# A hybrid diffusion backbone on one core: TensorE's list scheduler separates transposes, and the first stage's code is reordered

## The chip, the cores and the metric

The kernel runs on 1 core of a Trainium2 chip. Its time is the device time of one execution in microseconds; lower is better. The profile is one execution taken by the hardware profiler on that core.

## The reference, cut to what matters

Two layers, each an adaLN-modulated RMS norm, a wide input projection, three token mixers (RG-LRU, chunkwise retention, latent attention) and a gated merge. 256 latent tokens and 256 context tokens go through the same weights; D_MODEL is 1024. What the change touches is how the first lines are scheduled, and every transpose of the program.

```python
def _layer(x, xc, c, c_ctx, lp, rope_ret, rope_mla, with_ctx):
    mod = jax.nn.silu(c) @ lp['w_mod'] + lp['b_mod']
    mod_c = jax.nn.silu(c_ctx) @ lp['w_mod'] + lp['b_mod']
    shift, scale, gate = jnp.split(mod, 3, axis=-1)
    shift_c, scale_c, gate_c = jnp.split(mod_c, 3, axis=-1)
    h = _rms(x, lp['norm_gain']) * (1.0 + scale[:, None]) + shift[:, None]
    hc = _rms(xc, lp['norm_gain']) * (1.0 + scale_c) + shift_c
    (xa, ga, qb, kb, vb, gb, qd, kvd, kr, gc, gm) = _split_cols(h @ lp['w_in'])
    ...
    x = x + (gate[:, None] * _merge(lp, ya, yb, yc, ga, gb, gc, gm)).astype(x.dtype)
```

## The kernel before, in words

**Arithmetic.** Every f32 matrix is split into a rounded high part and a remainder, `hi` and `lo` (an ACT copy and a DVE subtraction), and each product is three matmuls (hi·hi, hi·lo, lo·hi, `mm3`). A matmul has a 128x128 stationary operand and 128 to 512 moving columns. A transpose is a TensorE instruction too: the data is the stationary operand, the identity (`ident`) moves, 128 columns. In the trace a transpose reads `mm<-ident,sm` or `mm<-ident,t`.

**Order.** Nothing is issued as it is written. All operations are recorded (`Recorder.add`), and `Recorder.schedule` then runs a list schedule over the five engines: each engine, when its modelled busy time is over, takes the ready operation that was recorded first (its `prio`), if the buffers that it writes are free within the windows of `WINDOW`, `FIRST` and `RESERVE`. The model's prices are in `_cost`; a transpose counts 107 ns there, a 512-column matmul 216 ns. The result is a fixed order per engine, which `emit` writes out at line 369; so nearly all instructions carry that one line. On the chip each engine works through its own order, and waits where an operand is not there.

**First stage.** Four blocks c = 0 to 3. `mod_pe` multiplies four weight tiles of `wmod` with the conditioning vector (`mm<-t,cz`, 16 instructions a block), ACT copies the bank, four small matmuls with `sel` bring the columns back (`mm<-sel,sm`), and DVE makes `sh` and `gt` from them (`put_columns`). `norm_begin` makes the normalized rows, each of four token tiles once; `norm_channels` transposes two channel tiles of a block (`mm<-ident,t`), scales them with `gt` and `sh` into `sm` and splits them into `hx`. `kv_project` of the block then multiplies `hx` with that block's split `wkv` tile (24 matmuls of 320 columns, `mm<-whi,hx` and `mm<-wlo,hx`). `rope_tables` loads two small tables (`mrope`, `grope`) and multiplies them into four tables `rt`; it stands behind the four blocks. All loads go out on SP's queue in the scheduled order. `t` in the trace is a buffer of the pool `t2` (21 buffers of 128x1024), used for the rows, the `wmod` tiles and most intermediates.

**Later.** Latent attention of layer 0 (about 40 to 200 us), LRU, retention and merge (to 870 us), latent attention of layer 1 (870 to 1000 us), then the rest. Transposes stand in both attentions (keys, queries, probabilities), in the retention heads, at the modulation of layer 1, at the norm between the layers and in the last merge.

Of the kernel before, what the change touches and what calls it, by code (L numbers as in the profile page):

```python
# [22 lines left out]
NTT = TOK // 128  # L23
# [128 lines left out]
class Recorder:  # L152
# [72 lines left out]
    def schedule(self):  # L225
# [28 lines left out]
        def switch(op):  # L254
            return op.table is not None and op.table != table[0]

        t = 0.0
        evn = 0
        left = len(ops)
        while left:  # L260
            progressed = True
            while progressed:
                progressed = False
                for e in engines:
                    if busy[e] > t:
                        continue
                    w = wait[e]
                    while w and w[0][0] <= t:
                        _, pr, k, op = heapq.heappop(w)
                        heapq.heappush(avail[e], (pr, k, op))  # L270
                    a = avail[e]
                    hold = []
                    pick = None
                    while a:
                        item = heapq.heappop(a)
                        op = item[2]
                        ok = True
                        need = {}
                        for b in op.allocs:
                            if b.live:  # L280
                                continue
                            need[b.tag] = need.get(b.tag, 0) + 1
                            spare = (FIRST if b.tag == "mm" and b.seq < 24 else RESERVE).get(b.tag, 0) if b.seq > nxt[b.tag] + need[b.tag] - 1 else 0
                            if free[b.tag] < need[b.tag] + spare or b.seq > nxt[b.tag] + WINDOW.get(b.tag, 0):
                                ok = False
                        if ok and pick is not None:
                            if not switch(op):
                                hold.append((pick.prio, id(pick), pick))
                                pick = op
                                break  # L290
                            ok = False
                        elif ok:
                            pick = op
                            if not switch(op):
                                break
                            limit = op.prio + SWITCH
                            continue
                        hold.append(item)
                        if pick is not None and item[0] > limit:
                            break  # L300
                    for item in hold:
                        heapq.heappush(a, item)
                    if pick is None:
                        continue
                    op = pick
                    for b in op.allocs:
                        if not b.live:
                            b.live = True
                            free[b.tag] -= 1
                            q = self.tags[b.tag]["queue"]  # L310
                            while nxt[b.tag] < len(q) and q[nxt[b.tag]].live:
                                nxt[b.tag] += 1
                    cost = op.cost
                    if switch(op):
                        cost += 1283.0
                        table[0] = op.table
                    op.start = t
                    busy[e] = t + cost
                    op.end = t + cost + op.lag
                    order.append(op)  # L320
                    left -= 1
                    evn += 1
                    heapq.heappush(events, (busy[e], evn, None))
                    evn += 1
                    heapq.heappush(events, (op.end, evn, op))
                    for s in op.succs:
                        if s.engine == e and e != "SP":
                            s.ready = max(s.ready, busy[e] + SELF[e])
                        else:
                            s.ready = max(s.ready, op.end + _latency(e, s.engine))  # L330
                        s.npred -= 1
                        if s.npred == 0:
                            heapq.heappush(wait[s.engine], (s.ready, s.prio, id(s), s))
                            evn += 1
                            heapq.heappush(events, (s.ready, evn, None))
                    progressed = True
            if not left:
                break
            if not events:
                self.stuck(nxt, free, wait, avail)  # L340
            t2, _, op = heapq.heappop(events)
            t = max(t, t2)
            batch = [op]
            while events and events[0][0] <= t:
                batch.append(heapq.heappop(events)[2])
            for op in batch:
                if op is not None:
                    for b in op.bufs:
                        b.users -= 1
                        if b.users == 0:  # L350
                            free[b.tag] += 1
# [97 lines left out]
def tile_hybrid(ctx, tc, ins, out):  # L449
# [265 lines left out]
        V.scalar_tensor_tensor(t, t, 1.0, ps, op0=ALU.add, op1=ALU.mult)  # L715
        return t

    def rope_tables(l):
        tabs = []
        mrope = small()[:, 0:384]  # L720
        S.dma_start(mrope, ins["mrope"])
        mrope = mrope.rearrange("p (a s d) -> p a s d", a=2, s=3)
        grope = small()[:, 0:128]
        S.dma_start(grope, ins["grope"][l])
        grope = grope.rearrange("p (a d) -> p a d", a=2)
        for i in range(2):
            for j in range(2):
                t = rec.tile(f"rt{i}{j}", [128, 3, 64], F32)
                V.tensor_tensor(t, mrope[:, j], grope[:, i:i + 1, :].to_broadcast([128, 3, 64]), op=ALU.mult)
                tabs.append(t)  # L730
        return tabs
# [459 lines left out]
    xn = {}  # L1191

    lat = Latents(0, None)
    xs = []
    for tt in range(NTT):
        xs.append(big(F32))
        S.dma_start(xs[tt], ins["xin"][tt])
    wm = {}
    for c in range(4):
        wm[c] = [big(F32) for _ in range(4)]  # L1200
        for kp in range(4):
            S.dma_start(wm[c][kp], ins["wmod"][0, 4 * c + kp])
        wkv = load_raw(ins["wkv"][0, c], 640)
        if c == 0:
            for tt in range(NTT):
                xn[tt] = norm_begin(xs[tt])
        mod_pe(0, c, wm, gt, sh)
        for kt in (2 * c, 2 * c + 1):
            norm_channels(xn, kt, gt, sh, hh, hl)
        lat.kv_project((c,), {c: wkv})  # L1210
    lat.tabs = rope_tables(0)
    sp = cload("sp", [128, DEPTH, 24])
    rrope = cload("rrope", [128, 2, 256])
    toep = cload("toep", [128, 384])
# [40 lines left out]
    for l in range(DEPTH):  # L1255
# [8 lines left out]
        hold = {}  # L1264
# [189 lines left out]
```

## Time and profile before

| | |
|---|---|
| median of 3 runs | 1396.25 us (1396.11 to 1398.47) |
| the profiled execution | 1396.45 us, of it the span 1394.1 us |
| TensorE (PE) | busy 1375.3 us, 99% of the span, 6926 matmuls |
| VectorE (DVE) | busy 1026.6 us, 74% |
| ScalarE (ACT) | busy 801.3 us, 57% |
| granted TensorE clock | 0.999 of full speed |
| HBM read | 167.86 MB, 121 GB/s over the span |

Matmuls are pipelined: the start of one and the modelled end of the one before overlap. So a duration of a matmul in the trace (some 390 ns for 512 columns) is not what it costs. The cost is read from the distance of starts, over a few instructions that are known by name.

### The profile page before, as it was taken

The numbers are of one execution on the slowest core, as the hardware profiler recorded it, in microseconds if no ns is written. First come the engines' busy times: TensorE is split into PE (matmuls) and PEld (weight loads), VectorE is DVE, ScalarE is ACT, GpSimd is POOL, SyncE is SP. The second block draws the span as 40 slices with busy tenths as digits, with TensorE's granted clock in tenths as the row PEclk, the third lists the DMA queues.
The fourth block names the chain that finished last, engine by engine and source line by source line (L and its number), as shares of the span: only waits on it lengthen the run. The fifth ranks groups of instructions, "written<-read, shape, count | busy, mean of one in ns | idle before, by whom it ended". The sixth has DMA issues, their size and how long they took to land.

```text
span 1394.1 us, 19215 instructions
## 1 busy us (share of the span) xinstructions
PE 1375.3 (99%) x6926; PEld 1162.4 (83%) x6926; DVE 1026.6 (74%) x2067; ACT 801.3 (57%) x1597; POOL 86.5 (6%) x109
## 2 busy tenths in 40 slices
PE   6999999999999999999999999999999999999998
PEld 4888888888888888888888888988888888888887
DVE  3699886676669656574884765899778898978755
ACT  4676665776678332153432226877686887945442
POOL 1131110000000000010000001312000000000000
PEclk9999999999999999999999999999999999999999
DMA  9412112223333433413344452333343444564662
GB/s 363 157 48 74 58 62 66 86 91 114 91 114 121 136 98 106 136 51 111 107 142 143 134 179 69 116 94 102 95 123 119 136 151 141 159 194 131 206 182 77
DMA packets 51070, 170.15 MB, mean 122 GB/s; under 512 B 6048, under 2 KB 7840, under 8 KB 50976
## 3 DMA queue, kind: packets, MB, share of 16 engines
q1 hardware_dynamic: 50976, 168.93, 38.4%
q8 instruction: 54, 0.88, 0.3%
q14 instruction: 40, 0.33, 0.1%
HBM read 167.86 MB, written 1.05 MB: 121 GB/s over the span
## 4 chain that ended last, share of the span: by engine, by line
PE 92%; DVE 3%; DMA 3%; ACT 1%; issue 0%; POOL 0%; SPq 0%; ACTq 0%; DVEq 0%; POOLq 0%
PE mm L369 92%; DMA t<-in_wmod_dram 1%; DVE sm L369 1%; DVE t L369 1%; DVE wlo L369 1%; DMA sm<-in_grope_dram 1%; ACT t L369 1%; DVE st L369 0%; DMA raw<-in_wmod_dram 0%; DMA t<-in_xin_dram 0%; ACT sm L369 0%; POOL st L369 0%; SPq L369 0%; ACT whi L369 0%; ACT hx L369 0%
## 5 line engine op out<-in xcount | busy, mean ns | idle before, releaser
L369 PE MATMUL mm<-hx,whi 128*128 128x512 f32 x1664 | 533.3, 393 | 0.0
L369 ACT CAST whi<-raw 128x1024 fp32r<-128x1024 f32 (+4 forms) x280 | 275.7, 995 | 342.6 <-PE mm L369 295.3
L369 DVE TENSOR_TENSOR wlo<-raw,whi 128x1024 fp32r<-128x1024 f32 (+4 forms) x280 | 318.7, 1143 | 143.9 <-ACT whi L369 141.9
L369 PEld LDWEIGHTS mm<-hx,whi 128*128 128x128 f32 x1664 | 309.5, 188 | 60.1
L369 PE MATMUL mm<-hx,wlo 128*128 128x512 f32 (+1 forms) x960 | 342.7, 362 | 0.0
L369 PE MATMUL mm<-whi,t 128*128 128x512 f32 (+1 forms) x656 | 208.9, 383 | 0.4 <-DVE t L369 0.4
L369 PEld LDWEIGHTS mm<-hx,wlo 128*128 128x128 f32 x960 | 180.2, 188 | 29.0
L369 PE MATMUL mm<-whi,hx 128*128 128x512 f32 (+2 forms) x672 | 198.0, 368 | 2.1 <-ACT hx L369 2.1
L369 POOL TENSOR_TENSOR st<-st,nhalf 128x2 f32<-128x2 f32 (+2 forms) x102 | 85.6, 846 | 1221.5 <-DVE st L369 1215.1
L369 PE MATMUL mm<-t,whi 128*128 128x512 f32 x512 | 160.2, 390 | 0.1
L369 PE MATMUL mm<-t,t 128*128 128x256 f32 (+1 forms) x912 | 156.2, 310 | 0.5 <-ACT t L369 0.5
L369 PEld LDWEIGHTS mm<-t,t 128*128 128x128 f32 x912 | 131.5, 189 | 12.9 <-DVE t L369 1.0
L369 PEld LDWEIGHTS mm<-whi,hx 128*128 128x128 f32 x672 | 122.8, 188 | 21.2 <-ACT hx L369 4.2
L369 PEld LDWEIGHTS mm<-whi,t 128*128 128x128 f32 x656 | 121.7, 188 | 18.8 <-DVE t L369 0.6
L369 PE MATMUL mm<-wlo,t 128*128 128x512 f32 (+1 forms) x328 | 125.4, 382 | 0.0
L369 PE MATMUL mm<-wlo,hx 128*128 128x512 f32 (+2 forms) x336 | 123.1, 368 | 0.0
L369 PEld LDWEIGHTS mm<-t,whi 128*128 128x128 f32 x512 | 95.9, 188 | 20.4 <-DVE t L369 0.5
L369 PE MATMUL mm<-t,wlo 128*128 128x512 f32 x256 | 99.7, 390 | 0.0
L369 ACT CAST t<-sm 128x256 fp32r<-128x256 f32 (+1 forms) x128 | 60.1, 486 | 64.1 <-DVE sm L369 60.8
L369 ACT ACTIVATE sm<-mm 128x128 f32<-128x128 f32 (+4 forms) x242 | 84.0, 364 | 20.8 <-PE mm L369 17.9
L369 ACT CAST t<-mm 128x256 fp32r<-128x256 f32 (+1 forms) x138 | 61.9, 471 | 30.9 <-PE mm L369 30.1
L369 DVE TENSOR_TENSOR t<-mm,t 128x512 fp32r<-128x512 f32 (+2 forms) x138 | 71.3, 530 | 8.2 <-ACT t L369 7.1
(106 smaller groups left out, 1507.9 us busy)
## 6 DMA issues: line engine op xcount, KB each, us to landing
raw<-in_wu_dram SPq DMA_DIRECT2D x224, 512.0 KB, 3.7
raw<-in_wmod_dram SPq DMA_DIRECT2D x32, 512.0 KB, 3.7
t<-in_wmod_dram SPq DMA_DIRECT2D x16, 512.0 KB, 9.6
t<-in_xin_dram SPq DMA_DIRECT2D x8, 512.0 KB, 6.4
raw<-in_wup_dram SPq DMA_DIRECT2D x8, 512.0 KB, 4.0
raw<-in_wlru_dram SPq DMA_DIRECT2D x16, 256.0 KB, 3.1
raw<-in_wqd_dram SPq DMA_DIRECT2D x8, 384.0 KB, 4.0
raw<-in_wup_dram SPq DMA_DIRECT2D x8, 384.0 KB, 3.4
```

Of the source, the lines that this page charges most:

```text
L369: getattr(eng[op.engine], op.method)(*[r(x) for x in op.args], **{k: r(v) for k, v in op.kwargs.items()})
```

## The change

Two parts. In `schedule`, TensorE remembers whether its last instruction was a transpose (`turned`). If it was, the first transpose that comes up is set aside (`stash`) and the search goes on among the ready operations; the transpose is taken if nothing else can go. A transpose that does not follow a transpose is priced at 30 ns in the model in place of 107. In the first stage, the two rope tables' loads (now one buffer, `rope_load`) are recorded ahead of the rows, `norm_begin` behind all `wmod` and `wkv` loads, and the projection of block c behind the modulation and norm of block c + 1.

```diff
+        turned = False
@@
                     pick = None
+                    stash = None
                     while a:
                         item = heapq.heappop(a)
                         op = item[2]
@@
+                        elif ok and e == "PE" and turned and op.method == "transpose":
+                            if stash is None:
+                                stash = item
+                            else:
+                                hold.append(item)
+                            continue
                         elif ok:
                             pick = op
@@
                     for item in hold:
                         heapq.heappush(a, item)
+                    if stash is not None:
+                        if pick is None:
+                            pick = stash[2]
+                        else:
+                            heapq.heappush(a, stash)
@@
                     cost = op.cost
+                    if e == "PE":
+                        if op.method == "transpose" and not turned:
+                            cost = 30.0
+                        turned = op.method == "transpose"
@@
-    def rope_tables(l):
+    def rope_load(l):
+        t = small()
+        S.dma_start(t[:, 0:384], ins["mrope"])
+        S.dma_start(t[:, 384:512], ins["grope"][l])
+        return t
+
+    def rope_tables(l, t=None):
         tabs = []
-        mrope = small()[:, 0:384]
-        S.dma_start(mrope, ins["mrope"])
-        mrope = mrope.rearrange("p (a s d) -> p a s d", a=2, s=3)
-        grope = small()[:, 0:128]
-        S.dma_start(grope, ins["grope"][l])
-        grope = grope.rearrange("p (a d) -> p a d", a=2)
+        t = t or rope_load(l)
+        mrope = t[:, 0:384].rearrange("p (a s d) -> p a s d", a=2, s=3)
+        grope = t[:, 384:512].rearrange("p (a d) -> p a d", a=2)
@@
     lat = Latents(0, None)
+    rload = rope_load(0)
     xs = []
@@
-    wm = {}
+    wm, wkv = {}, {}
     for c in range(4):
         wm[c] = [big(F32) for _ in range(4)]
         for kp in range(4):
             S.dma_start(wm[c][kp], ins["wmod"][0, 4 * c + kp])
-        wkv = load_raw(ins["wkv"][0, c], 640)
-        if c == 0:
-            for tt in range(NTT):
-                xn[tt] = norm_begin(xs[tt])
+        wkv[c] = load_raw(ins["wkv"][0, c], 640)
+    for tt in range(NTT):
+        xn[tt] = norm_begin(xs[tt])
+    for c in range(4):
         mod_pe(0, c, wm, gt, sh)
         for kt in (2 * c, 2 * c + 1):
             norm_channels(xn, kt, gt, sh, hh, hl)
-        lat.kv_project((c,), {c: wkv})
-    lat.tabs = rope_tables(0)
+        if c:
+            lat.kv_project((c - 1,), wkv)
+    lat.kv_project((3,), wkv)
+    lat.tabs = rope_tables(0, rload)
```

What that does to the fixed orders is shown at three places. Counted over the whole of TensorE's order, there are 522 transposes before and after. Before they stand in 169 runs (6 of one transpose, 105 of two, 29 of four, 14 of eight, 15 of other lengths), so that 353 of them follow another transpose. After they stand in 472 runs, 453 of them of one transpose, and 50 follow another. The number of matmuls does not change.

**TensorE, a norm between the layers** (`norm_half`): eight transposes of one row tile, beside matmuls of the next output rows (`hx` is the stationary operand there, `whi` and `wlo` the split weights). Before:

```order
L369 MATMUL mm<-t_6912,whi 128x512 x2
L369 MATMUL mm<-t_6912,wlo 128x512
L369 MATMUL mm<-ident,t_6360 128x128 x8
L369 MATMUL mm<-hx,whi 128x512 x2
L369 MATMUL mm<-hx,wlo 128x512
L369 MATMUL mm<-hx,whi 128x512 x2
```

After, the same eight transposes begin behind the same matmul, with one 512-column matmul between each two:

```order
L386 MATMUL mm<-t_6909,whi 128x512 x2
L386 MATMUL mm<-t_6909,wlo 128x512
L386 MATMUL mm<-ident,t_6359 128x128
L386 MATMUL mm<-hx,whi 128x512
L386 MATMUL mm<-ident,t_6359 128x128
L386 MATMUL mm<-hx,whi 128x512
L386 MATMUL mm<-ident,t_6359 128x128
L386 MATMUL mm<-hx,wlo 128x512
L386 MATMUL mm<-ident,t_6359 128x128
L386 MATMUL mm<-hx,whi 128x512
```

The run of eight became eight runs of one; the matmuls in between are those that stood behind the run.

**VectorE, the first stage**: the four products for `rt` need the rope tables, `st`, `sh` and `gt` are a block's modulation columns, `sm` its scaled channels. Before, in the third block:

```order
L369 TENSOR_TENSOR hx<-sm,hx 128x512 x2
L369 TENSOR_TENSOR rt_384<-sm 128x192
L369 TENSOR_TENSOR st<-mm,cols 128x8
L369 TENSOR_TENSOR wlo<-raw,whi 128x640
L369 COPY sh<-st 128x4
L369 SCALAR_TENSOR_TENSOR gt<-st,cols 128x4
L369 TENSOR_TENSOR rt_404<-sm 128x192
L369 TENSOR_SCALAR sm<-mm,gt,sh 128x256 x2
```

After, the same products stand at the start of the program, ahead of the norm's first operation; the split of the first `wkv` tile (`wlo`) stands ahead of the third row tile's norm (`t_181`):

```order
L386 COPY cz<-cf 128x2x8
L386 TENSOR_TENSOR rt_134<-sm 128x192
L386 TENSOR_TENSOR rt_136<-sm 128x192
L386 TENSOR_TENSOR rt_140<-sm 128x192
L386 TENSOR_TENSOR rt_142<-sm 128x192
L386 TENSOR_SCALAR st<-st 128x1
L386 TENSOR_SCALAR t_156<-t_121,st 128x1024
L386 TENSOR_SCALAR st<-st 128x1
L386 TENSOR_SCALAR t_169<-t_125,st 128x1024
L386 TENSOR_SCALAR st<-st 128x1
L386 TENSOR_TENSOR wlo<-raw,whi 128x640
L386 TENSOR_SCALAR t_181<-t_138,st 128x1024
```

The rope products left the third block, and a wait for a `wkv` tile came into the norm.

**ScalarE, the first stage**: the norms of the four row tiles (`ACTIVATE t,st<-t`), the cast of the first `wkv` tile (`CAST whi<-raw`), and the copy of the first modulation bank (`COPY sm<-mm`). Before:

```order
L369 ACTIVATE t_133,st<-t_117 128x1024
L369 ACTIVATE t_139,st<-t_120 128x1024
L369 ACTIVATE t_146,st<-t_131 128x1024
L369 ACTIVATE t_162,st<-t_136 128x1024
L369 CAST whi<-raw 128x640
L369 COPY sm<-mm 128x512
```

After:

```order
L386 ACTIVATE t_156,st<-t_121 128x1024
L386 ACTIVATE t_169,st<-t_125 128x1024
L386 ACTIVATE t_181,st<-t_138 128x1024
L386 CAST whi<-raw 128x640
L386 ACTIVATE t_195,st<-t_144 128x1024
L386 COPY sm<-mm 128x512
```

The cast moved ahead of the fourth norm. On TensorE the `sel` matmuls of a block's modulation moved from behind the projection of the block before it into that projection (behind its 4th, 11th and 11th matmul for blocks 1, 2 and 3), and the last `cz` matmuls of block 1 moved from behind the projection of block 0 to ahead of it.

## Rows read from the trace of the kernel before

**Rows 1.** The page, part 1: busy time, share, instructions

```profile
PE 1375.3 (99%) x6926; PEld 1162.4 (83%) x6926; DVE 1026.6 (74%) x2067; ACT 801.3 (57%) x1597; POOL 86.5 (6%) x109
```

**Rows 2.** Busy by stretch: length, PE, PEld, DVE, ACT, POOL, clock, DMA share, GB/s

```profile
21.00:38.70 17.70, 14.72 (x107) 10.35 (x105) 8.33 (x21) 7.44 (x14) 0.00 (x0) 1.00 1.04 397
...
85.00:126.40 41.40, 40.39 (x228) 33.69 (x226) 40.09 (x132) 26.33 (x96) 9.47 (x9) 1.00 0.26 79
```

**Rows 3.** Timeline, PE alone, no transposes near: start us, duration us, what

```profile
300.26 0.62 PE L369 MATMUL mm<-hx,whi 128*128 128x512 f32 x2
...
300.94 0.62 PE L369 MATMUL mm<-hx,whi 128*128 128x512 f32 x2
```

**Rows 4.** Timeline, PE alone, around a run of eight transposes

```profile
746.93 0.40 PE L369 MATMUL mm<-t,wlo 128*128 128x512 f32 x1
747.17 1.04 PE L369 MATMUL mm<-ident,t 128*128 128x128 f32 x8
747.96 0.70 PE L369 MATMUL mm<-hx,whi 128*128 128x512 f32 x2
748.50 0.39 PE L369 MATMUL mm<-hx,wlo 128*128 128x512 f32 x1
```

**Rows 5.** Timeline, PE alone, around a run of two

```profile
104.19 0.62 PE L369 MATMUL mm<-hx,whi 128*128 128x512 f32 x2
104.65 0.39 PE L369 MATMUL mm<-hx,wlo 128*128 128x512 f32 x1
104.88 0.38 PE L369 MATMUL mm<-ident,sm 128*128 128x128 f32 x2
105.02 0.71 PE L369 MATMUL mm<-hx,whi 128*128 128x512 f32 x2
105.56 0.40 PE L369 MATMUL mm<-hx,wlo 128*128 128x512 f32 x1
```

**Rows 6.** Timeline, PE and weight loads (PEld), around one transpose between matmuls

```profile
58.31 0.34 PE L369 MATMUL mm<-whi,hx 128*128 128x384 f32 x1
...
58.49 0.27 PE L369 MATMUL mm<-ident,sm 128*128 128x128 f32 x1
58.49 0.19 PEld L369 LDWEIGHTS mm<-whi,hx 128*128 128x128 f32 x1
58.52 0.42 PE L369 MATMUL mm<-whi,hx 128*128 128x384 f32 x1
...
58.77 0.34 PE L369 MATMUL mm<-wlo,hx 128*128 128x384 f32 x1
```

**Rows 7.** The chain that ended last, first 45 us: start us, us, what

```profile
26.93 8.50 DMA sm<-in_grope_dram
...
38.72 6.43 PE mm L369 x45
```

**Rows 8.** Timeline of the first stage, all engines

```profile
9.86 1.06 ACT L369 ACTIVATE t<-t 128x1024 f32<-128x1024 f32 x1
...
15.82 0.72 ACT L369 CAST whi<-raw 128x640 fp32r<-128x640 f32 x1 [4.82 <-DMA raw<-in_wkv_dram]
...
16.64 0.58 ACT L369 COPY sm<-mm 128x512 f32<-128x512 f32 x1
...
21.08 0.39 PE L369 MATMUL mm<-whi,hx 128*128 128x320 f32 x1
...
30.23 0.41 PE L369 MATMUL mm<-whi,hx 128*128 128x320 f32 x1 [0.48 <-ACT hx L369]
...
33.85 0.95 PE L369 MATMUL mm<-sel,sm 128*128 128x2 f32 x8
...
35.22 1.92 PE L369 MATMUL mm<-t,cz 128*32 128x512 f32 x16
```

**Rows 9.** DMA issues, first 45 us: what, count, KB each, median us to landing

```profile
sm<-in_mrope_dram SPq DMA_DIRECT2D x1, 192.0 KB, 9.6
...
sm<-in_grope_dram SPq DMA_DIRECT2D x1, 64.0 KB, 8.5
```

## The prediction

> **What bounds the kernel now.** I read the page first: TensorE is busy 99% of the span and no other engine over 74% [rows 1], at full clock. So time goes where TensorE's order gets longer or shorter, or where TensorE starts later. Then the stretches: before 38.7 us TensorE waits (of 21.0 to 38.7 us it works 14.72 of 17.70), later hardly at all, even between 85 and 126 us, where DVE is busy 40.09 of 41.40 us and TensorE still 40.39 [rows 2]. The chain of waits says the same: ahead of 38.72 us it runs over DMAs, DVE and ACT, at 38.72 us it enters TensorE [rows 7]. So two questions decide: what a transpose costs by itself and in a run, and when TensorE starts its unbroken work.
>
> What an instruction costs is the distance of starts. Three 512-column matmuls take 0.68 us (300.26 to 300.94), 227 ns each [rows 3]. A run of eight: from 746.93 to 748.50 us there are three such matmuls and eight transposes, 1.57 − 0.68 = 0.89 us, **111 ns a transpose** [rows 4]. A run of two: from 104.19 to 105.56 us there are five matmuls and two transposes, 1.37 − 1.135 = 0.235 us, 118 ns each [rows 5].
>
> **Part 1, transposes set apart.** It removes nothing and adds nothing: 522 transposes before and after. It makes 303 runs more (472 less 169). The scheduler's price of 30 ns says that a transpose between matmuls costs 80 ns less. One of the six single transposes before shows what it does cost. From 58.31 to 58.77 us there are two 384-column matmuls and one transpose. The matmul ahead of it takes 0.18 us to the transpose's start (58.49). The next matmul is recorded 0.03 us behind the transpose, which looks like a price of 30 ns; but the one behind that starts only 0.25 us later. Taken over the three, 0.46 − 2×0.175 = **0.11 us** [rows 6]. The same rows show why: the weight load of the matmul behind the transpose starts with the transpose (both 58.49), so what the matmul ahead hid was the transpose's own load, and the load behind is not hidden by a transpose that streams 128 columns only.
>
> So I take no gain from it. What it adds is a border: a run of n costs n×p + f. With p = 109 ns, the eight give f = 0.89 − 0.87 = 0.02 us, the two give 0.235 − 0.218 = 0.017 us, the single one about nothing (0.11 − 0.109). Ends: 0 and 17 ns for each of 303 runs, 0 to 5.2 us. Among the new runs 215 stand behind a 512-column matmul, the rest behind narrower ones like the single one here; and where one matmul alone stands between two transposes (334 places after) two borders share it. I take 5 ns, the side of the row that has the form of the new runs: **+1.5 us**. Below zero, only if a load is hidden that rows 6 show unhidden; that is a rival, below.
>
> The Trainium skill ("TensorE: Matmul & The Clock Gate", section "Part 2: What happens when you issue a matmul") says that weight loads are pulled ahead of matmuls in flight, so that the next tile's weights load while this tile's matmul runs. The trace agrees for the transpose's own load, not for the one behind it (0.11 us for the single transpose [rows 6]). By the page's gap of N/2.4 + 2.5 ns a transpose with both loads hidden would be an estimate of 56 ns, and 303 of them 16 us less.
>
> **Part 2, the first stage.** The rope tables' loads, 192 + 64 KB [rows 9], now stand ahead of the rows and all `wmod` tiles on SP's queue; at 397 GB/s [rows 2] all that follows lands 0.66 us later. In return nothing waits for them at 35.4 us, where they landed (26.93 + 8.50 [rows 7]) and DVE stood ahead of the third block's columns. ACT's order costs more. The cast of the first `wkv` tile waited for its DMA until 15.82 us [rows 8]; now until 16.5, and behind it stand the fourth norm (1.06 us and 0.2 for its sum) and the copy of the first modulation bank, which goes from 16.64 to about 18.8 us. DVE's third and fourth norm wait behind the same tile's split: its cast ends at 17.2, the split and the third norm take 1.6, the fourth norm is ready at some 20.7 us. From there the columns, scaling and cast take 2.8 us, as from the copy's end to the first projection before (17.22 to 21.08, less the `sel`). Projection 0 starts near **23.5** instead of 21.08 us.
>
> Then the moved pieces pay it back. Projection 0 has 24 matmuls, 3.6 us (30.23 to 33.85 [rows 8]), holds block 1's `sel` (0.95 us) and about 0.5 us of wait for the copy: to 28.6. Block 2's `cz` matmuls, 1.92: 30.5. Projection 1 starts there, close to 30.23 before, since its columns came during projection 0. It holds block 2's `sel` and four transposes (3.6 + 0.95 + 0.45): 35.5. Block 3's `cz`, 1.9: 37.4. By then block 2's channels are there (its `sel` ends near 33.1, and columns, scaling and cast take 2.8 to 3 us: 36), and projection 2 starts at **37.4 instead of 38.72 us**. What TensorE has left from there is the same in both (projections 2 and 3, block 3's `sel` and eight transposes, all of the later work). So **−1.3 us**. Ends: −3.0, all that TensorE idles from 21.0 to 38.7 us [rows 2], and +0.7, if the late loads are the last word. The rope products (DVE, 1.3 us) are hidden at the start, where DVE waits for the rows; without that cover they would cost what they cost before.
>
> **The rest of the order** moves with the prices; I find no wait that it adds by name. In the stretch where DVE is full, TensorE loses 1.0 us now [rows 2]; a different interleaving may win that or lose as much again. Middle: 0.
>
> Sum against the profiled execution: 1396.45 − 1.3 + 1.5 = 1396.65 us. Its time lies 0.2 above the median of the three, so in terms of medians **1396.5 us**.
>
> **Rivals.**
> *Hidden transposes.* If a separated transpose costs what its start shows, 30 ns [rows 6], 303 of them save 80 ns each, 24 us: 1396.25 − 24 − 1.3 = 1371 us. For it: the distance between the two starts. Against it: the next distance of the same rows, which gives it all back. This is also the case in which the change does what its price says. The Trainium skill's rule on loads pulled ahead (same page and section as above) stands beside it.
> *A full border.* If each new run costs what the run of two costs between 512-column matmuls, 17 ns [rows 5], that is 5.2 us: 1396.25 − 1.3 + 5.2 = 1400.1 us, slower. It decides from 13 ns a border on (2.8 + 1.3 us over 303). For it: 329 of the 472 runs stand behind 512 columns. Against it: the single transpose with no border to see.
> *The front pays in full.* If projection 2 starts as soon as TensorE's work before it allows, all 3.0 us are won, and with borders at 1 ns it is 1396.25 − 3.0 + 0.3 = 1393.5 us, at the edge of faster. Against it: ACT's late fourth norm.
> *No effect at all*: the front's gain eaten by its later loads, borders free: 1396.9 us, inside the forecast's own range.
>
> **How the numbers follow.** Some 0.2%, 2.8 us, is what a measurement of this kernel can tell from no change. My forecast, between 1393.5 and 1399 us, 0.54; the full border (or a wait that the new order adds in the full stretches) 0.23; the front in full 0.16; hidden transposes 0.07. So faster 0.23, same 0.54, slower 0.23. The range goes from the front in full with the won 1.0 us of the full stretch (1392.5) to the full border with 1.0 lost and the front at nothing (1402.5); hidden transposes lie outside.
>
> **What would show it.** In the changed profile, TensorE's busy share stays 99% and the span within 3 us. Around the norm between the layers, eight transposes and seven matmuls should take 8×0.11 + 7×0.227 = 2.5 us; 1.8 us would say that they are hidden. A matmul's weight load should start with the transpose ahead of it, and not before. The fourth norm on ACT should stand near 17.3 us, projection 0 start near 23.5 and projection 2 near 37.4 us; if projection 0 is as late as that and projection 2 later than 38.7, my paying back is wrong. Wrong altogether would be a span under 1385 us, or new waits on TensorE of over 1 us in the attention stages.

## The result and the profile after

The changed kernel takes **1411.95 us** (median of 4, 1411.88 to 1412.77), the kernel before, run beside it, 1396.58 us (1396.11 to 1398.47). The ratio is **1.0108**, 95% interval 1.0096 to 1.0121: slower by some 15 us, outside the forecast's range. The profiled execution has a span of 1409.8 us against 1394.1, 15.7 us more, at the same clock.

The page, part 1, of the changed kernel, as [rows 1] of before. DVE (1026.6 us before) and ACT (801.3) do the same work; TensorE's share falls from 99% to 98%:

```profile
PE 1383.6 (98%) x6926; PEld 1157.5 (82%) x6926; DVE 1027.7 (73%) x2067; ACT 804.3 (57%) x1597; POOL 85.9 (6%) x109
```

Where it went is read from places that both programs have: the first transposes of a stage, and projection 2's first matmul. First TensorE's timeline of before (start, duration, what), then of after:

```profile
522.24 0.38 PE L369 MATMUL mm<-ident,sm 128*128 128x128 f32 x2
...
848.91 1.03 PE L369 MATMUL mm<-ident,t 128*128 128x128 f32 x8
...
1091.39 0.38 PE L369 MATMUL mm<-ident,sm 128*128 128x128 f32 x2
```

```profile
41.15 0.42 PE L386 MATMUL mm<-whi,hx 128*128 128x320 f32 x1
...
531.38 0.28 PE L386 MATMUL mm<-ident,sm 128*128 128x128 f32 x1
...
858.48 0.27 PE L386 MATMUL mm<-ident,t 128*128 128x128 f32 x1
...
1106.86 0.27 PE L386 MATMUL mm<-ident,sm 128*128 128x128 f32 x1
```

| stretch, up to | before | after | added |
|---|---|---|---|
| first stage: projection 2 starts ([rows 7]) | 38.72 | 41.15 | 2.4 |
| latent attention, layer 0: first of the later transposes | 522.24 | 531.38 | 6.7 |
| 64 transposes in runs of two and eight, nearly all set apart after; the norm between the layers starts | 848.91 | 858.48 | 0.4 |
| that norm and the attention of layer 1 | 1091.39 | 1106.86 | 5.9 |
| the rest (end of span) | 1394.1 | 1409.8 | 0.2 |

So four fifths lie in the two attention stretches with the norm between them. TensorE waits there by name, which it hardly did before. The list of TensorE's waits from 45 to 210 us (engine and line waited for: us in total, times, longest), before and after:

```profile
PE mm L369 <- ACT t L369: 0.5, 1, 0.5
PE mm L369 <- DVE t L369: 0.4, 1, 0.4
```

```profile
PE mm L386 <- DVE t L386: 2.3, 3, 1.1
PE mm L386 <- ACT t L386: 1.6, 2, 1.1
PE mm L386 <- ACT sm L386: 0.8, 2, 0.4
PE mm L386 <- DVE sm L386: 0.6, 2, 0.4
```

Busy time by stretch after, in the columns of [rows 2], for the two stretches that it names:

```profile
21.00:38.70 17.70, 17.70 (x107) 11.35 (x107) 8.41 (x22) 7.27 (x14) 0.00 (x0) 1.00 1.03 403
85.00:126.40 41.40, 39.26 (x216) 31.87 (x215) 38.47 (x129) 26.02 (x100) 9.11 (x10) 1.00 0.20 66
```

From 21.0 to 38.7 us TensorE no longer stands at all, and still projection 2 starts later: there it has too much to do. Where DVE is full it loses 2.1 us instead of 1.0. How such a wait comes about is seen in TensorE's timeline behind this stretch:

```profile
124.63 0.27 PE L386 MATMUL mm<-ident,sm 128*128 128x128 f32 x1
124.66 0.48 PE L386 MATMUL mm<-wlo,t 128*128 128x512 f32 x1
...
126.00 0.87 PE L386 MATMUL mm<-t,t 128*128 128x256 f32 x6
127.51 1.10 PE L386 MATMUL mm<-t,t 128*128 128x256 f32 x7 [0.63 <-DVE t L386]
...
130.26 0.44 PE L386 MATMUL mm<-ident,sm 128*128 128x128 f32 x2 [1.09 <-DVE t L386]
...
134.82 0.39 PE L386 MATMUL mm<-t,t 128*128 128x256 f32 x1 [1.12 <-ACT t L386]
```

Up to 126 us every transpose has a weight matmul beside it. From 126 to 135 us hardly anything but the attention's own pieces stands in TensorE's order, and it stands 0.63, 1.09 and 1.12 us for DVE and ACT. How many matmuls with `whi` fall into these two stretches (length, PE busy with them and their number, clock, DMA share, GB/s), before and after:

```profile
118.00:126.00 8.00, 4.15 (x12) 1.00 0.51 158
126.00:135.00 9.00, 4.05 (x13) 1.00 0.01 3
```

```profile
118.00:126.00 8.00, 6.82 (x20) 1.00 0.25 87
126.00:135.00 9.00, 1.75 (x5) 1.00 0.18 59
```

It is 25 in both. Before they are spread evenly; after, 20 of them are gone when the waits come.

The norm between the layers shows a wait of another kind. Its timeline, TensorE and ACT:

```profile
858.48 0.27 PE L386 MATMUL mm<-ident,t 128*128 128x128 f32 x1
...
858.82 0.27 PE L386 MATMUL mm<-ident,t 128*128 128x128 f32 x1
...
859.13 0.46 ACT L386 ACTIVATE sm<-mm,sh,gt 128x128 f32<-128x128 f32 x1 [3.52 <-PE mm L386]
...
859.64 0.33 PE L386 MATMUL mm<-ident,t 128*128 128x128 f32 x1 [0.31 <-ACT sm L386]
...
860.51 0.33 PE L386 MATMUL mm<-ident,t 128*128 128x128 f32 x1 [0.31 <-ACT sm L386]
```

Two transposes into the bank go through. Then the plan lets ACT read the first quarter, and the third transpose, into another quarter of that bank, waits 0.31 us for ACT; the fourth waits for the next read. In before the four stood together ahead of all reads.

### The profile page after: what moved, and what is told of

Read it like the earlier page. It is cut to its first block, busy times and chain, and to the rows that moved or that the text cites. A ratio compares the mean times of both kernels' runs of the same rounds, so it can differ in the third digit from the quotient of the medians.

```text
span 1409.8 us, 19196 instructions
## 1 busy us (share of the span) xinstructions
PE 1383.6 (98%) x6926; PEld 1157.5 (82%) x6926; DVE 1027.7 (73%) x2067; ACT 804.3 (57%) x1597; POOL 85.9 (6%) x109
## 4 chain that ended last, share of the span: by engine, by line
PE 96%; DVE 2%; ACT 1%; DMA 1%; SPq 0%; issue 0%; POOL 0%; ACTq 0%
PE mm L386 96%; DVE sm L386 1%; DVE t L386 1%; ACT sm L386 1%; DMA t<-in_wmod_dram 1%; DVE st L386 0%; ACT t L386 0%; SPq L386 0%; POOL st L386 0%; DVE wlo L386 0%; ACTq L386 0%
## 5 line engine op out<-in xcount | busy, mean ns | idle before, releaser
L386 PE MATMUL mm<-hx,whi 128*128 128x512 f32 x1664 | 539.5, 397 | 0.1
L386 PE MATMUL mm<-hx,wlo 128*128 128x512 f32 (+1 forms) x960 | 346.8, 367 | 0.0
L386 PE MATMUL mm<-whi,t 128*128 128x512 f32 (+1 forms) x656 | 213.1, 391 | 0.5 <-ACT sm L386 0.4
L386 PE MATMUL mm<-whi,hx 128*128 128x512 f32 (+2 forms) x672 | 200.9, 372 | 1.2 <-ACT sm L386 1.2
L386 PE MATMUL mm<-ident,sm 128*128 128x128 f32 x410 | 106.2, 273 | 1.9 <-DVE t L386 1.1
```

Of the source, the lines that this page charges most:

```text
L386: getattr(eng[op.engine], op.method)(*[r(x) for x in op.args], **{k: r(v) for k, v in op.kwargs.items()})
```

## The experiments

My theories: (R) the rule loses, since it spends ready matmuls ahead of transposes; (P) the price of 30 ns misleads the plan; (F) the first stage's new code loses, or only the rule's alternation in it; (B) the norm's bank waits. The first stage's code and schedule() can be exchanged between the two kernels. All times follow; "waits" are TensorE's by name in the two attention stretches, 41 to 210 and 845 to 1012 us.

| kernel | median us | ratio to before, interval | waits us |
|---|---|---|---|
| before | 1396.6 to 1397.4 | | 0.9, 0 |
| changed | 1411.95 | 1.0108 [1.0096, 1.0121] | 5.3, 3.1 |
| first stage alone | 1396.4 | 0.9995 [0.9985, 1.0005] | 0.9, 0 |
| rule and price alone | 1413.2 | 1.0114 [1.0099, 1.0129] | 5.3, 3.0 |
| rule alone | 1409.71 | 1.0088 [1.0073, 1.0103] | 3.1, 2.8 |
| price alone | 1397.24 | 0.9995 [0.9986, 1.0005] | 1.4, 0 |
| changed, banks whole | 1412.32 | 1.0103 [1.0088, 1.0118] | 5.2, 3.2 |
| rule, norms left out | 1403.54 | 1.0044 [1.0030, 1.0058] | 3.1, 0.8 |
| first stage alone, norms back | 1394.52 | 0.9981 [0.9973, 0.9990] | 0.9, 0 |
| the same, rope loads back | **1393.2** | **0.9971 [0.9960, 0.9981]** | 0.9, 0 |
| matmul ahead, runs kept | 1399.57 | 1.0016 [1.0007, 1.0026] | 2.8, 0.4 |
| traced prices, no rule | 1411.99 | 1.0108 [1.0093, 1.0123] | 3.7, 1.0 |
| traced prices and rule | 1409.92 | 1.0090 [1.0074, 1.0107] | 2.6, 0.7 |
| changed, norms back | 1408.21 | 1.0080 [1.0065, 1.0095] | 5.3, 3.0 |

### The parts of the change, one by one

The new first stage with schedule() of before:

> The new code of the first stage (rope loads first, cast and block order turned) with the scheduler of before; nothing else is changed. If the miss in front (projection 2 at 41.15 us, forecast 37.4, before 38.72) comes from the alternation of cz matmuls and single transposes that the new rule makes there, this kernel shows what the prediction put on the code alone: projection 0 near 23.5, projection 2 near 37.4 us, and 1.3 us less than before, 1395.2 us. If the code itself is to blame (the fourth norm standing behind the cast on ACT), projection 2 stands near 41 us here too and the time is 2.3 us over before, 1398.9 us. The rest of the order should cost nothing in either case, within 1 us.

The old first stage with schedule() of after:

> The first stage of before with the new scheduler, rule and price. If the loss is the scheduler's (theory: 15.4 us less the 2.3 of the front, thus some 13 us), 1409.5 us, with the same waits on TensorE between 50 and 200 us (about 7 us) and in the norm between the layers (about 3 us). If the loss came from the two parts together (a first stage that ends later and shifts what follows), it is under 6 us here: 1396.6 to 1402 us.

From it the rule without the price:

```
-                        if op.method == "transpose" and not turned:
-                            cost = 30.0
                         turned = op.method == "transpose"
```

> The first stage of before; of the scheduler the rule alone (a transpose does not follow a transpose while another matmul is ready), with the old price of 107 ns for every transpose. If the rule loses the time, by spending ready matmuls as separators where DVE and ACT are full and by spreading transposes among DVE's and ACT's reads, 1406 to 1410 us. If the price misleads the plan (it believes TensorE to be 80 ns per separated transpose ahead of where it is, so that matmuls are placed where their data is not there yet), the rule with the true price costs the borders only: 1.6 to 2 us by the excess behind transposes in the changed kernel's trace, 1398.5 us.

And the price without the rule:

```
-                        elif ok and e == "PE" and turned and op.method == "transpose":
-                            if stash is None:
-                                stash = item
-                            else:
-                                hold.append(item)
-                            continue
```

> The first stage of before; of the scheduler the price of 30 ns alone, for a transpose that does not stand behind a transpose, without the rule. By the theory that the rule loses the time this kernel is like before within 1.5 us: 1395 to 1398 us. By the theory that the wrong price misleads the plan it loses most of the 13 us, though fewer transposes carry the price here (about 169 runs instead of 472), so at least 4 us: 1400 to 1409 us.

The scheduler loses it all (1.0114), the rule by itself most of it (1.0088): theory R. The price by itself costs nothing, so P alone is out; but on top of the rule it takes another 0.0026, some 3.6 us, in the attention of layer 0: TensorE's waits there are 5.3 us with it and 3.1 without. That fits the plan's error, since with the rule 303 more transposes carry a price that is 77 ns below the old one. TensorE's waits from 45 to 210 us with the rule alone:

```profile
PE mm L384 <- ACT sm L384: 1.8, 2, 0.9
PE mm L384 <- DVE t L384: 0.9, 3, 0.4
PE mm L384 <- DVE sm L384: 0.4, 1, 0.4
```

The first stage came out between my two numbers, and its timeline says that neither was the reason:

```profile
12.92 4.39 PE L369 MATMUL mm<-t,cz 128*32 128x512 f32 x12 [12.92 <-DMA t<-in_wmod_dram]
17.24 0.90 PE L369 MATMUL mm<-ident,t 128*128 128x128 f32 x3
...
39.58 0.42 PE L369 MATMUL mm<-whi,hx 128*128 128x320 f32 x1
```

TensorE's first instruction is a modulation matmul that waits until 12.92 us for its weights; the first transposes stand behind it at 17.24. From there it works without a pause. In before they came first:

```profile
8.84 1.12 PE L369 MATMUL mm<-ident,t 128*128 128x128 f32 x4 [8.84 <-DVE st L369]
```

Of the 2.4 us that projection 2 came late in the changed kernel, 0.9 are the code's and 1.6 the rule's (41.15 less 39.58), by these two profiles. The split is rough: up to the first `sel` matmul both issue the same order, and it starts at 20.52 us here and 19.83 there (the three transposes take 0.90 us here, 0.55 there), so some 0.6 us belong to neither (last section). By the times, the new first stage alone costs nothing that can be told from before (0.9995).

### The first stage: which piece

In the new code the norms' tiles are recorded behind those of all sixteen weight tiles, and the planner gives tiles of one pool out nearly in that order (a window of 12). The next kernel puts the norms back; the second takes the early rope loads out of it as well:

```
         wkv[c] = load_raw(ins["wkv"][0, c], 640)
-    for tt in range(NTT):
-        xn[tt] = norm_begin(xs[tt])
+        if c == 0:
+            for tt in range(NTT):
+                xn[tt] = norm_begin(xs[tt])
```

> The new first stage with the scheduler of before, and one part of it undone: the four norms are again written right behind the first block's loads instead of behind those of all four blocks. With the norms written last, TensorE's first instruction was a modulation matmul that waited for its weights until 12.92 us, and the first transpose came at 17.24 us; projection 2 started at 39.58 us. If the place of the norms in the text is the cause (their tiles queue behind all sixteen weight tiles), TensorE starts near 9.5 us with transposes here, projection 0 near 23.5 us, projection 2 near 37.4 us, as predicted for the change, and the time is 1.3 to 3 us under before: 1394 to 1396 us. If the early rope loads or the modulation standing ahead of the projection are the cause, projection 2 stays near 39.6 us and the time at 1396.5 to 1397.5 us.

```
-    rload = rope_load(0)
...
-    lat.tabs = rope_tables(0, rload)
+    lat.tabs = rope_tables(0)
```

> As the kernel with the norms back in their place, and the rope tables' loads back behind the weights too: of the first stage's change only the modulation of the next block ahead of a projection is left. If this reordering is what gains, 1393.5 to 1395.5 us, and by the 0.66 us that the early rope loads cost all later loads it is 0.5 us better than with them. If the wait for the rope tables (1.57 us of TensorE at 38.72 us before, behind a load that landed at 35.43) is what can be gained, it is still there, projection 2 starts near 38.7 us and the time is that of before within 1 us.

TensorE's first transpose, projection 0 and projection 2 with the norms back, then the first transpose and projection 2 with the rope loads back too:

```profile
10.29 1.11 PE L369 MATMUL mm<-ident,t 128*128 128x128 f32 x4 [10.29 <-DVE st L369]
...
24.41 0.41 PE L369 MATMUL mm<-whi,hx 128*128 128x320 f32 x1
...
37.73 0.42 PE L369 MATMUL mm<-whi,hx 128*128 128x320 f32 x1
```

```profile
8.94 1.11 PE L369 MATMUL mm<-ident,t 128*128 128x128 f32 x4 [8.94 <-DVE st L369]
...
36.00 0.42 PE L369 MATMUL mm<-whi,hx 128*128 128x320 f32 x1
```

The place of the norms is the cause: with them back, projection 2 starts 1.0 us earlier than in before, near the 37.4 us that the prediction had for the change, though not for its reasons (see below). The early rope loads help nothing and cost 1.3 us of the time (1394.52 against 1393.2) and 1.7 us of that start, of which 1.35 are there at the first transpose already. Without them projection 2 starts at 36.00 us, and TensorE waits for nothing after 18 us in the first stage: the modulation ahead of the projection also covers the late rope tables. This is the version that beats both kernels, by 0.29% against before.

The same undone in the changed kernel itself:

> The changed kernel (rule, price, new first stage) with one thing undone: the four norms are written right behind the first block's loads again. If their place is what cost the first stage, TensorE starts with transposes near 10.3 us instead of 12.84, the alternation of single transposes and modulation matmuls before projection 0 shrinks to two pairs, projection 2 starts near 37.9 us instead of 41.15, and the time is some 3 us less than that of the changed kernel: 1409 us. If the rule makes the first stage slow whatever the place of the norms, projection 2 stays beyond 39.5 us and the time is within 1.5 us of the changed kernel.

```profile
37.17 0.41 PE L386 MATMUL mm<-whi,hx 128*128 128x320 f32 x1
```

Projection 2 starts 4.0 us earlier and the time falls by 3.7 us. The rule's 1.6 us in the first stage are not seen here (37.17 us against 37.73 with the norms back and the scheduler of before; up to the first `sel` the two orders are the same, and there it is 0.7 us ahead already): two modulation matmuls between single transposes took 1.24 us a pair, and with the transposes done early no such pair is left ahead of projection 0.

### The norm's banks

To the changed kernel, where a bank's four reads have just been recorded behind its four transposes:

```
+        for op in rec.ops[-4:]:
+            op.preds.update(rec.ops[-8:-4])
```

> The changed kernel with one more condition in the norm between the layers: ACT and DVE read none of the four quarters of a bank before all four transposes of the bank are done. The transposes stay set apart by matmuls. In the changed kernel the third and fourth transpose of a bank wait for ACT, 3.1 us in all between 858 and 873 us. If these waits come from ACT's reads of the first quarters standing between the transposes of the same bank, they are gone here and the span is 3 us shorter (1409 us instead of 1412), with the chain behind a bank starting 0.5 to 0.7 us later. If they come from something else (ACT late with earlier work, or the separators' own data), TensorE still waits some 3 us there and the time is that of the changed kernel.

The expectation put the norm's waits at 3.1 us; the norm itself, 853 to 875 us, has 1.9 us of them, and a wait of 1.2 us at 998 us makes up the 3.1. In this kernel the 1.9 us are gone: between 853 and 875 us TensorE waits for nothing. So reads between transposes of one bank are what made them wait. But little is won: from the norm's first transpose to the last place of the table above it is 247.7 us instead of 248.4, and the time does not show it (1.0103 against 1.0108). From 845 to 1012 us there are 3.2 us of waits again, elsewhere, the longest where a projection waits for what ACT makes of the last bank. TensorE, then ACT:

```profile
888.16 0.42 PE L386 MATMUL mm<-whi,hx 128*128 128x320 f32 x1 [1.27 <-ACT hx L386]
```

```profile
887.47 0.63 ACT L386 CAST hx<-sm 128x512 fp32r<-128x512 f32 x1
```

### The rule by place, and what of it loses

The rule alone, only for transposes of sm tiles:

```
-                        elif ok and e == "PE" and turned and op.method == "transpose":
+                        elif ok and e == "PE" and turned and op.method == "transpose" and op.args[1].buf.tag == "sm":
```

> The rule alone with the old price and the old first stage, and the rule for the transposes of the latent attention and of the smaller mixers only (operand in an sm tile, 410 of the 522); the 112 transposes of the norms keep their old order. If each place loses by itself: the first stage (3.6 us in the kernel with the rule everywhere) and the norm between the layers (about 4 us) are back to those of before, what stays is the attention stretches, 3 to 5 us, and the borders, about 1 us: 1401 to 1403 us. If the attention stretches lose only because the stages ahead of them end late, they too are back and the time is within 1.5 us of before.

The attention of layer 0 keeps its 3.1 us of waits, and the second stretch falls from 2.8 to 0.8 us. So the attention loses by itself, and by the difference so do the places with the norms' transposes: with these left out about half of the rule's loss stays (1.0044 against 1.0088). One part of the expectation fell: in this profile the first stage is not back, though TensorE's order is that of before up to 53 us. See the last section.

The rule turned round: a ready matmul ahead of a run, and the run kept whole:

```
-                        elif ok and e == "PE" and turned and op.method == "transpose":
+                        elif ok and e == "PE" and not turned and not paid and op.method == "transpose":
...
+                        paid = op.method != "transpose" and stash is not None
```

> The rule turned round, with the old price and the old first stage: when a transpose comes up behind something else, another ready matmul goes ahead of it, once, and the transposes of a run then stay together (157 runs instead of 169 before, 8 of a norm in a row). So later work is pulled ahead of transposes as by the rule, about half as often, and nothing is set apart. If the rule loses because matmuls that the attention stretches need later are spent ahead of transposes, TensorE gets new waits between 50 and 200 us here too, 1.5 to 3 us, with none in the norm between the layers: 1398.5 to 1401 us. If it loses because transposes are set apart (borders, and banks that are handed to and fro between TensorE and ACT), the time is that of before within 1 us.

It loses 0.16%, and TensorE waits between 45 and 210 us nearly as long as with the rule:

```profile
PE mm L385 <- DVE sm L385: 1.7, 3, 0.7
PE mm L385 <- DVE t L385: 0.8, 2, 0.5
...
```

Nothing is set apart here, so setting apart is not what makes these waits; what this kernel shares with the rule is that later matmuls are put ahead of transposes that DVE and ACT depend on. The norm has no waits here, as expected.

Last, whether the rule must lose, or a better informed plan would bear it. The planner's prices set to the trace, then the rule for sm tiles on top:

```
-            return 107.0, 0.0
+            return 109.0, 0.0
...
-        return max(passes * n / 2.4, 27.0 if passes == 1 else 211.0) + 2.7, 0.0
+        return max(passes * n / 2.4, 27.0 if passes == 1 else 211.0) + 13.4, 0.0
```

> The kernel before with the planner's prices set to the trace: a 512-column matmul 227 ns instead of 216 (N/2.4 + 13.4 ns, from the 227 and 174 ns of 512 and 384 columns), a transpose 109 instead of 107 ns. No rule, the old first stage. It is the ground for the next kernel. Nothing new is computed and nothing waits by itself, so only the interleaving moves: 1394 to 1401 us. If TensorE's waits in the attention stretches of before (0.9 us) come from prices that are too low, they go, and it is at the lower end.

> The kernel with the traced prices, and the rule for the transposes of the attention and of the smaller mixers, as in the kernel that lost 6 us with the old prices. If the rule by itself loses (it spends ready matmuls, whatever the plan knows), this is again 4 to 6 us over the kernel with the traced prices alone. If the waits come in because the plan believes TensorE to be 5% faster than it is and so doesn't see that the matmuls run out, a plan with the right prices places them better, and the two kernels agree within 1.5 us, with under 1 us of waits on TensorE between 50 and 200 us.

True prices alone lose 1.08%, far more than I expected, with TensorE standing in many places. On top of that plan the rule costs nothing that can be measured (1.0090 against 1.0108, intervals overlapping). So the rule does not lose in every plan. But neither theory is borne out: the plan had the waits already (3.7 us from 41 to 210 us), and with the rule they are 2.6 us where I expected under 1. Whether better prices would save a good plan stays open. What the pair shows is how much hangs on the plan: drawing it anew with other prices cost as much as the whole change. So a rival stays: that part of the rule's loss comes from redrawing a plan that happened to be good, whatever the rule. Against it stands the price alone, which redraws the order from the 168th matmul on and costs nothing (0.9995), but one such kernel does not exclude it.

## Why the prediction was wrong

**The border: the mechanism right, the size near.** Eight transposes apart, seven 512-column matmuls between them, no wait: the last of them on TensorE's timeline of after (the first, at 531.38, stands above):

```profile
533.80 0.27 PE L386 MATMUL mm<-ident,sm 128*128 128x128 f32 x1
```

From the first it is 2.42 us for seven pairs, 346 ns each; less 227 ([rows 3]) a transpose costs 119 ns. So *hidden transposes* is refuted: the estimate by the rule of the Trainium skill ("TensorE: Matmul & The Clock Gate", "Part 2: What happens when you issue a matmul") of 56 ns and 16 us less isn't seen; the load behind a transpose stays in the open, as [rows 6] said. The border is 10 ns here against the 5 that I took, thus up to 3.0 us for 303 instead of 1.5; from 522 to 849 us, where no wait is added, 64 transposes in 20 runs became 61 runs and cost 0.4 us more, again some 10 ns for each new run. Both lie within my ends.

**The rest of the order: the step that failed, some 10 us.** I wrote "I find no wait that it adds by name" and took the middle at 0, with 1 us either way from the 1.0 us that TensorE lost in the DVE-full stretch. That bound held what TensorE loses under the old order, not what it can lose. In a stretch where DVE is busy 40.09 of 41.40 us [rows 2], TensorE goes on only because other matmuls are ready; the rule takes just these, at each transpose, and puts them ahead of what feeds DVE and ACT. The prediction's own sign for "wrong altogether", new waits of over 1 us in the attention stages, is what came: 1.09 and 1.12 us. The rival "a wait that the new order adds in the full stretches" was named, but tied to a full border's price of 5.2 us, a third of what came. By name the waits of the two attention stretches are 7.5 us more (5.3 and 3.1 against 0.9). A wait costs more than its recorded idle: in the norm the step from the second transpose to the third is 0.82 us (858.82 to 859.64), an undisturbed one 0.34 (858.48 to 858.82), so 0.48 us for an idle of 0.31. If that holds for all 16 waits after, against 2 before, it adds 2.4 us, an estimate from this one place. Then waits, border (3.0) and first stage (2.4) make 15.3 of the 15.7 us.

**The norm.** Eight transposes and seven matmuls in 2.5 us were right where nothing reads their bank meanwhile (531.38 to 533.80 us and one more). In the norm they were not: two transposes and a wait. I looked at what a transpose costs TensorE and not at who reads the bank between two of them.

**The first stage: the wrong engine.** It came out 2.4 us longer, where I had taken 1.3 off and 0.7 on as the worst. The fourth norm stands at 18.00 us (I said 17.3) and the copy of the first modulation bank behind it, as forecast. But I timed projection 0 by ACT and DVE alone. TensorE's rows after:

```profile
12.84 4.14 PE L386 MATMUL mm<-t,cz 128*32 128x512 f32 x12 [12.84 <-DMA t<-in_wmod_dram]
16.91 0.55 PE L386 MATMUL mm<-ident,t 128*128 128x128 f32 x3
...
20.98 1.04 PE L386 MATMUL mm<-t,cz 128*32 128x512 f32 x2
...
22.22 1.05 PE L386 MATMUL mm<-t,cz 128*32 128x512 f32 x2
...
27.87 0.39 PE L386 MATMUL mm<-whi,hx 128*128 128x320 f32 x1
```

Its queue begins with twelve modulation matmuls, so the transposes of before's 8.84 us come from 16.91 on, in part single ones alternating with pairs of modulation matmuls at 1.24 us a pair (20.98 to 22.22), where sixteen in a row take 1.92 [rows 8]. Projection 0 starts at 27.87 instead of my 23.5, projection 2 at 41.15 instead of 37.4. The paying back itself was near: from projection 0 to projection 2 it is 13.3 us here, 13.9 in the sum. With the norms back in their place, projection 0 and projection 2 come within a microsecond of my times (24.41 and 37.73), but that is luck: the fourth norm stands at 11.48 us there, and my 23.5 was reasoned from its standing behind the cast.

**The early rope loads** I charged with 0.66 us, 256 KB at 397 GB/s. They cost twice that: ACT's first norm, which waits for the first row tile, starts at 7.62 us in the changed kernel instead of 6.03, and with the norms back at 7.47 us with the early loads, 6.12 without. GB/s in 40 slices of 0 to 45 us, before and after:

```profile
GB/s 0 7 138 157 397 422 408 411 415 430 422 408 396 416 404 411 411 405 400 408 415 411 410 393 413 415 419 390 388 364 357 393 393 385 409 290 40 46 325 219
```

```profile
GB/s 0 7 124 237 164 339 393 397 426 422 415 422 408 399 417 408 408 408 415 399 410 408 408 412 393 418 408 408 408 406 363 396 396 399 363 66 18 29 182 255
```

From the third slice on, four slices of 1.1 us move 138, 157, 397 and 422 GB/s before and 124, 237, 164 and 339 after, some 0.28 MB less, and 0.26 MB of the rest are the rope tables. Together that is 1.4 us at 397 GB/s, close to the 1.35 and 1.6 us of the first norm. Why the rate comes up later with these loads in front, the rows don't show.

## What to carry to other kernels

Before a scheduler separates instructions "with whatever is ready", ask what that ready work was going to cover: in a stretch where another engine is full it is the reserve that keeps the bound engine going, and taking it early returns as waits. Read what stands at the head of the bound engine's own queue before timing it by its suppliers; where tiles come from a shared pool in order of recording, moving a piece of code behind many loads also moves its tiles. And taking away one wait (the banks, 1.9 us) gains little (0.7 us) while the next consumer of the same chain is as late.

## What the hardware showed that I had not expected

The same order of TensorE's instructions didn't give the same first stage in every profile. With the rule for sm tiles alone, TensorE's order is that of before up to 53 us, yet the modulation matmuls of block 2 took 2.66 us instead of 1.92. Their row, and the busy times of the stretch around them in the columns of [rows 2], 0.65 the granted clock:

```profile
29.50 2.66 PE L384 MATMUL mm<-t,cz 128*32 128x512 f32 x16 [0.26 <-DVE st L384]
```

```profile
29.50:33.00 3.50, 3.50 (x19) 1.33 (x20) 3.06 (x7) 2.53 (x5) 0.00 (x0) 0.65 1.02 402
```

The clock is 0.65 on the mean of these 3.5 us, so most of it at the lower of the two levels, 1.2 GHz; TensorE had just stood 0.69 and 0.26 us for ACT and DVE, as in before, where it stayed at 1.00. Projection 2 then started at 40.46 us. The clock also fell in the first stage of four more kernels with the old code there (rule and price, the rule alone, the matmul ahead, traced prices and rule), not in that of before, of the price alone and of the traced prices alone. These five are the ones with some form of the rule; how it could act there, ahead of the first matmul that it moves, the rows don't show, and five against three may be chance. What decides it stays open. For such kernels the first stage of one profile is uncertain by some 1.7 us, and the timed medians are the better ground: the rule for sm tiles is 7.8 us longer than before by its span, 6.1 by its median.

A second difference of this kind touches all kernels. TensorE's first instructions last nearly twice as long as later ones (in the changed kernel a modulation matmul 1.06 us at 14.0 us, 0.59 us at 17.8 us), which fits the lower of the two clock levels; the granted clock is not recorded that early. When this ends differs from profile to profile. The changed kernel and the one with the banks whole have the same order of TensorE up to the norm between the layers, yet projection 2 starts at 41.15 us in the one and here in the other:

```profile
42.05 0.42 PE L386 MATMUL mm<-whi,hx 128*128 128x320 f32 x1
```

So differences of under a microsecond between first stages of single profiles say little, the split of the 2.4 us above among them.
